# RMSNorm with repeated rows on one core: loads from SyncE and stores from ScalarE, two hardware DMA queues in place of one

## The chip, the cores and the metric

The kernel runs on one core of one Trainium2 chip. The metric is the device time of one execution in microseconds (us); lower is better. An execution more than 1.5% above the fastest of its kernel counts as slow and is left out of the ratios. The rounds of runs fell on several chips, so kernels of different rounds are compared by their ratios to the kernel before, run in the same round. A *load* here is a DMA from HBM to SBUF, a *store* one from SBUF to HBM. SyncE, ScalarE (ACT) and GpSimd (POOL) can issue DMAs; VectorE is DVE. A `q` after an engine's name in a profile line means its sequencer.

## The reference

```python
x: (8, 512, 2048) float32, gamma: (2048,) float32
x_rep = np.repeat(x, 2, axis=1)                       # each row twice
rms = np.sqrt((x_rep ** 2).mean(axis=-1, keepdims=True) + 1e-6)
return (x_rep / rms * gamma).astype(np.float32)       # (8, 1024, 2048)
```

33.6 MB are read and 67.1 MB written, with very little arithmetic per byte.

## The kernel before

The 4096 rows of x are handled in eight tiles of 512 rows, four rows to each of 128 partitions. A tile's buffer `y` holds the output (eight rows per partition); the input is loaded into its upper half. There are three such buffers, so the load of tile i+2 reuses the buffer of tile i-1 and must wait until that tile's store has landed.

```python
K = 4                                           # rows per partition
rows = ctx.enter_context(tc.tile_pool(name="rows", bufs=3))
...                                             # cut
def load(i, parts=1):
    y = rows.tile([P, K * R, D], f32, name="y")
    ...                                         # cut: in `parts` pieces
        nc.sync.dma_start(out=y[:, at : at + step, :], in_=x_t[i, :, k : k + step, :])   # L52
...                                             # cut: load(0), gamma, load(1), load(2)
for i in range(ntiles):
    y = ys[i]
    for k in range(K):
        xk = y[:, K * (R - 1) + k, :]
        y0, y1 = y[:, R * k, :], y[:, R * k + 1, :]
        ...                                     # cut: small tiles
        nc.scalar.activation(out=sq[:], in_=xk, func=Act.Square, accum_out=ss[:])       # L71
        nc.scalar.activation(out=rms[:], in_=ss[:], func=Act.Sqrt, ...)                 # L73
        nc.vector.reciprocal(out=rstd[:], in_=rms[:])                                   # L75
        nc.vector.scalar_tensor_tensor(out=y0, in0=xk, scalar=rstd[:], in1=gamma_b[:], ...)  # L76
        if k == K - 1:
            nc.vector.tensor_copy(out=y1, in_=y0)                                       # L81
        else:
            nc.scalar.copy(out=y1, in_=y0)                                              # L83
    nc.sync.dma_start(out=out_t[i], in_=y.rearrange("p j d -> p (j d)"))                # L84
    if i >= 1 and i + 2 < ntiles:
        load(i + 2)
```

Of the kernel before, what the change touches and what calls it, by code (L numbers as in the profile page):

```python
# [1 line left out]

# [4 lines left out]


@with_exitstack
def kernel(  # L10
    ctx: ExitStack,
    tc: tile.TileContext,
    x: bass.AP,
    gamma: bass.AP,
    out: bass.AP,
):
    nc = tc.nc
    P = nc.NUM_PARTITIONS
    f32 = mybir.dt.float32
    Act = mybir.ActivationFunctionType  # L20
    Alu = mybir.AluOpType

    B, S, D = x.shape
    Bo, So, Do = out.shape
    R = So // S
    assert R == 2 and D == Do and B == Bo and So == S * R
    eps = 1e-6
    inv_d = 1.0 / float(D)


    K = 4
    N = B * S
    assert N % (P * K) == 0
    ntiles = N // (P * K)
    x_t = x.rearrange("b s d -> (b s) d").rearrange("(n p k) d -> n p k d", p=P, k=K)
    out_t = out.rearrange("b s d -> (b s) d").rearrange("(n p j) d -> n p (j d)", p=P, j=K * R)

    singles = ctx.enter_context(tc.tile_pool(name="singles", bufs=1))
    rows = ctx.enter_context(tc.tile_pool(name="rows", bufs=3))
    junk = ctx.enter_context(tc.tile_pool(name="junk", bufs=1, space=bass.MemoryType.PSUM))  # L40
    small = ctx.enter_context(tc.tile_pool(name="small", bufs=8))

    ys = []

    def load(i, parts=1):


        y = rows.tile([P, K * R, D], f32, name="y")
        step = K // parts
        for k in range(0, K, step):  # L50
            at = K * (R - 1) + k
            nc.sync.dma_start(out=y[:, at : at + step, :], in_=x_t[i, :, k : k + step, :])  # L52
        ys.append(y)

    load(0, parts=K)
    gamma_b = singles.tile([P, D], f32, name="gamma_b")
    nc.scalar.dma_start(out=gamma_b[0:1, :], in_=gamma.partition_broadcast(1))
    nc.gpsimd.partition_broadcast(out_ap=gamma_b[:], in_ap=gamma_b[0:1, :])  # L58
    eps_t = singles.tile([P, 1], f32, name="eps_t")
    nc.vector.memset(eps_t, eps)  # L60
    load(1)
    load(2)
# [6 lines that stand above are left out]
            sq = junk.tile([P, D], f32, name="sq")  # L69
            ss = small.tile([P, 1], f32, name="ss")  # L70
            nc.scalar.activation(out=sq[:], in_=xk, func=Act.Square, accum_out=ss[:])  # L71
            rms = small.tile([P, 1], f32, name="rms")
            nc.scalar.activation(out=rms[:], in_=ss[:], func=Act.Sqrt, scale=inv_d, bias=eps_t[:])  # L73
            rstd = small.tile([P, 1], f32, name="rstd")
            nc.vector.reciprocal(out=rstd[:], in_=rms[:])  # L75
            nc.vector.scalar_tensor_tensor(  # L76
                out=y0, in0=xk, scalar=rstd[:], in1=gamma_b[:],
                op0=Alu.mult, op1=Alu.mult,
            )
            if k == K - 1:  # L80
                nc.vector.tensor_copy(out=y1, in_=y0)  # L81
            else:
                nc.scalar.copy(out=y1, in_=y0)  # L83
        nc.sync.dma_start(out=out_t[i], in_=y.rearrange("p j d -> p (j d)"))  # L84
        if i >= 1 and i + 2 < ntiles:
            load(i + 2)


# [1 line left out]
_INS = ['x', 'gamma']  # L90
_OUTS = [((8, 1024, 2048), 'float32')]


# [23 lines left out]
```

## Time and profile before

| | before |
|---|---|
| time, median of the first 3 runs | 240.29 us (239.80 to 241.39) |
| span of the profiled run | 239.1 us |
| DMA queue q1, share of 16 engines | 98.3% |
| ACT busy, DVE busy | 49%, 37% |

These lines of the page show the span, the DMA engines' busy tenths in 40 slices of 6 us, the one queue that carries the traffic, and, for each group of DMA issues, the issuing sequencer, the count, the size and the median time from issue to landing.

```profile
span 239.1 us, 293 instructions
...
DMA  7999998989899999899898999899989899898984
...
q1 hardware_dynamic: 2736, 100.66, 98.3%
...
y<-in_x_dram SPq DMA_DIRECT2D x7, 4096.0 KB, 38.8
...
out_dram<-y SPq DMA_DIRECT2D x8, 32.0
```

The DMA engines are the limit: no slice between the first and the last is below 8. Next, SyncE's own waits (who waited for whom: total us, times, longest):

```profile
SPq L84 <- DVE y L81: 161.7, 8, 28.9
SPq L52 <- DMA out_dram<-y: 38.8, 5, 18.4
```

SyncE has nothing else to do, so it stands at each store (L84) until VectorE's last copy of the tile (L81) is done, and issues it at once. Five loads (L52) wait for the landing of the store that frees their buffer. The end of the run in the timeline (start, duration, engine, line, operation; in brackets the idle time before it and what ended it):

```profile
185.41 1.23 DVE L81 COPY y<-y 128x2048 f32<-128x2048 f32 x1
186.70 0.33 SPq L84 DMA_DIRECT2D out_dram<-y  x1
199.38 1.88 ACT L71 ACTIVATE sq<-y 128x2048 f32<-128x2048 f32 x1 [14.53 <-DMA y<-in_x_dram]
...
215.97 0.33 SPq L84 DMA_DIRECT2D out_dram<-y  x1
```

Tile 6 is done at 186.6 us and its store is issued at 186.70; the last load lands at 199.38, when ACT begins tile 7.

For the accounting below I added up the durations of all packet records of the trace (packets of 8 KB and more, without the queue that loads instructions) and divided by 16. The span is then this sum plus the engines' mean idle time: before, 239.07 = 234.81 + 4.26.

### The profile page before, as it was taken

The numbers are of one execution on the slowest core, as the hardware profiler recorded it, in microseconds if no ns is written. First come the engines' busy times: TensorE is split into PE (matmuls) and PEld (weight loads), VectorE is DVE, ScalarE is ACT, GpSimd is POOL, SyncE is SP. The second block draws the span as 40 slices with busy tenths as digits, with TensorE's granted clock in tenths as the row PEclk, the third lists the DMA queues.
The fourth block names the chain that finished last, engine by engine and source line by source line (L and its number), as shares of the span: only waits on it lengthen the run. The fifth ranks groups of instructions, "written<-read, shape, count | busy, mean of one in ns | idle before, by whom it ended". The sixth has DMA issues, their size and how long they took to land.

```text
span 239.1 us, 293 instructions
## 1 busy us (share of the span) xinstructions
DVE 88.8 (37%) x73; ACT 116.3 (49%) x122; POOL 2.5 (1%) x5
## 2 busy tenths in 40 slices
DVE  0449759590000085400863016820168202591000
ACT  2998999950000299104990059800598006970000
POOL 4000000000000000000000000000000000000000
DMA  7999998989899999899898999899989899898984
GB/s 262 426 454 439 439 439 351 526 351 526 351 428 439 493 395 451 384 411 510 362 515 351 439 439 506 373 422 433 493 384 471 362 461 461 384 482 384 493 384 175
DMA packets 2741, 100.69 MB, mean 421 GB/s; under 512 B 306, under 2 KB 306, under 8 KB 306
## 3 DMA queue, kind: packets, MB, share of 16 engines
q1 hardware_dynamic: 2736, 100.66, 98.3%
q14 instruction: 3, 0.02, 0.0%
q10 hardware_dynamic: 2, 0.01, 0.0%
HBM read 33.56 MB, written 67.11 MB: 421 GB/s over the span
## 4 chain that ended last, share of the span: by engine, by line
DMA 68%; ACT 13%; DVE 8%; SPq 1%; issue 1%
DMA y<-in_x_dram 41%; DMA out_dram<-y 27%; ACT sq L71 7%; DVE y L76 6%; ACT y L83 5%; DVE y L81 2%; SPq L52 1%; ACT rms L73 1%; DVE rstd L75 0%; SPq L84 0%
## 5 line engine op out<-in xcount | busy, mean ns | idle before, releaser
L71 ACT ACTIVATE sq<-y 128x2048 f32<-128x2048 f32 x32 | 59.7, 1865 | 92.5 <-DMA y<-in_x_dram 92.5
L76 DVE SCALAR_TENSOR_TENSOR y<-y,rstd,gamma_b 128x2048 f32<-128x2048 f32 x32 | 75.3, 2352 | 1.2
L75 DVE RECIPROCAL rstd<-rms 128x1 f32<-128x1 f32 x32 | 5.1, 159 | 124.8 <-ACT rms L73 124.8
L83 ACT COPY y<-y 128x2048 f32<-128x2048 f32 x24 | 44.7, 1890 | 3.2 <-DVE y L76 3.2
L81 DVE COPY y<-y 128x2048 f32<-128x2048 f32 x8 | 9.8, 1226 | 0.3
L73 ACT ACTIVATE rms<-ss,eps_t 128x1 f32<-128x1 f32 x32 | 9.4, 293 | 0.7
L71 ACT ACTIVATION_READ_ACCUMULATOR sq<-y 128x1 f32 x32 | 6.0, 186 | 0.0
L58 POOL PARTITION_BROADCAST gamma_b<-gamma_b x1 | 2.3, 2293 | 2.1 <-DMA gamma_b<-in_gamma_dram 2.1
L71 ACT ACT_TABLE_LOAD x1 | 1.3, 1283 | 1.3 <-PEq L101 1.3
L73 ACT ACT_TABLE_LOAD x1 | 1.3, 1283 | 0.0
L60 DVE MEMSET eps_t<- 128x1 f32 x1 | 0.1, 59 | 0.8 <-PEq L101 0.8
L101 POOL MEMSET const-bfloat16-1.0<- 128x1 bf16 x1 | 0.1, 101 | 0.0
L101 POOL MEMSET const-uint8-127<- 128x1 uint8 x1 | 0.1, 101 | 0.0
L101 POOL MEMSET const-float32-0.0<- 128x1 f32 x1 | 0.1, 98 | 0.2 <-issue 0.2
L101 POOL MEMSET const-float32-1.0<- 128x1 f32 x1 | 0.1, 99 | 0.0
## 6 DMA issues: line engine op xcount, KB each, us to landing
y<-in_x_dram SPq DMA_DIRECT2D x7, 4096.0 KB, 38.8
y<-in_x_dram SPq DMA_DIRECT2D x4, 1024.0 KB, 8.0
out_dram<-y SPq DMA_DIRECT2D x8, 32.0
gamma_b<-in_gamma_dram ACTq DMA_DIRECT2D x1, 8.0 KB
```

Of the source, the lines that this page charges most:

```text
L52: nc.sync.dma_start(out=y[:, at : at + step, :], in_=x_t[i, :, k : k + step, :])
L58: nc.gpsimd.partition_broadcast(out_ap=gamma_b[:], in_ap=gamma_b[0:1, :])
L60: nc.vector.memset(eps_t, eps)
L71: nc.scalar.activation(out=sq[:], in_=xk, func=Act.Square, accum_out=ss[:])
L73: nc.scalar.activation(out=rms[:], in_=ss[:], func=Act.Sqrt, scale=inv_d, bias=eps_t[:])
L75: nc.vector.reciprocal(out=rstd[:], in_=rms[:])
L76: nc.vector.scalar_tensor_tensor(out=y0, in0=xk, scalar=rstd[:], in1=gamma_b[:], op0=Alu.mult, op1=Alu.mult,)
L81: nc.vector.tensor_copy(out=y1, in_=y0)
L83: nc.scalar.copy(out=y1, in_=y0)
L101: nc = _bacc.Bacc("TRN2", target_bir_lowering=False, num_devices=1)
```

## The change

The intent: loads wait for buffers and stores wait for compute, so give each its own queue, and neither stands behind the other. The Trainium skill gives this advice ("Perfetto Trace Analysis", DMA Optimizations: one engine for inputs and another for outputs "may make sense").

```diff
-        nc.sync.dma_start(out=out_t[i], in_=y.rearrange("p j d -> p (j d)"))
+        nc.scalar.dma_start(out=out_t[i], in_=y.rearrange("p j d -> p (j d)"))
         if i >= 1 and i + 2 < ntiles:
             load(i + 2)
```

## The prediction

> **What bounds the kernel now.** The DMA engines. In the page's queue part one queue, q1, carries 100.66 MB and its packets take 98.3% of sixteen engines' span (239.1 us). ACT is busy 49%, DVE 37%. Loads are 4 MB in 32 KB packets, stores 8 MB in 64 KB packets. In the trace's packet records the median load packet took 1213 ns, the median store packet 2418 ns: 27.0 and 27.1 GB/s per engine, 432 and 434 GB/s over sixteen. Both directions run alike, so I read this as the engine's own limit. The Trainium skill ("DMA: Bandwidth & Descriptors", Where 436 GB/s comes from) puts the ceiling at 435.2 GB/s; the trace agrees within 1%.
>
> Floor, an estimate from those packets: (512 x 309 ns + 896 x 1213 ns + 1024 x 2418 ns) / 16 = 232.6 us. The records sum to 234.8 us. The other 4.3 us of the span are start and last completion. So at most 2.2 us of stretched packets lie open to a reordering.
>
> **What the change does.** It removes nothing: same bytes, packets and engines. Eight stores leave SyncE (332 ns each) for ScalarE. The same page (Issuing engines are not separate DMA queues) says that such DMAs interleave on the same engines and save only issue time, which is not on the critical path here. In SyncE's waits, 161.7 us go to the last VectorE copy of a tile and 38.8 us (5 times) to a store landing before a load. All five late loads are held by the landing of the store that frees their buffer, not by their place behind a store on SyncE. A second queue cannot issue them earlier.
>
> **What moves.** In one queue the order is strict: store, load, store, load, one pair per 29.2 us (load issues at 101.4, 130.5, 159.7 us in the timeline). With two queues a load and the next store share the engines. If they alternate packet by packet, both finish together some 29 us after the load's issue: loads land after 20 to 30 us instead of 38.8, stores after 35 to 45 us instead of 32. Buffers come free at the same pace.
>
> Does it run dry? A tile computes in about 16.5 us (111.1 to 127.6 us). Before, the last load lands at 199.4, the last store is issued at 216.0, and the store ahead of it needs until about 219: some 3 us to spare. After, I work out the last load landing at 196 to 198 us, its store ready at 213 to 215, the previous store ending at about 216. Still full, with 2 to 3 us to spare; a later last load would cost its excess directly.
>
> ScalarE pays 8 x 0.33 us for issues and waits for VectorE's copy (1.2 us) before the next tile's squares: about 1.7 us per tile, where tiles follow without a gap. It has 92.5 us of waits for loads to absorb it.
>
> **Prediction.** 240 us, unchanged. 8 in 10: 237.8 to 242.5. Faster by over 2%: 0.04 (needs 235.5, below floor plus start and end). Within 2%: 0.90. Slower by over 2%: 0.06.
>
> **What would show it.** Queue part: q1 keeps about 33.6 MB, a ScalarE queue takes 67.1 MB; their shares sum to 97 to 99%. Mean stays 418 to 425 GB/s. Late loads land 20 to 30 us after issue. SyncE's waits are nearly all for stores landing. No slice of the DMA row between start and end falls below 8.
>
> **What would make it wrong.** Faster, if two queues on one engine overlap reads and writes and move more than 27.1 GB/s. Slower, if switching between reads and writes stretches the packets, or if stores starve the last load and the queue runs dry before the last store.

## The result, and the profile after

| | before | after |
|---|---|---|
| median | 240.07 us (4 runs) | 250.18 us (4 runs) |
| ratio | | 1.043, interval 1.036 to 1.050 |
| span of the profiled run | 239.07 us | 248.05 us |
| packet durations / 16 | 234.81 us | 238.05 us |
| DMA engines' mean idle time | 4.26 us | 10.00 us |

A ratio is the mean time of one kernel's fast runs over that of the other's of the same rounds, so it is not quite the ratio of the medians. The change is slower by 4%. The 9.0 us of the span are 5.7 us of idle DMA engines and 3.2 us of packets that took longer.

The page after, the lines that answer to those of before:

```profile
span 248.0 us, 297 instructions
...
DMA  7999999999899899999998989999989947797993
...
q10 hardware_dynamic: 1154, 67.12, 62.5%
q1 hardware_dynamic: 1584, 33.56, 33.5%
...
y<-in_x_dram SPq DMA_DIRECT2D x7, 4096.0 KB, 20.8
...
out_dram<-y ACTq DMA_DIRECT2D x8, 28.4
```

The traffic split as intended. But in the slice from 198 to 205 us (the 4 ahead of 7797993) the DMA engines are 4 tenths busy, and the two next are at 7. In the packet records no packet at all is in flight from 202.8 to 207.7 us. SyncE's wait line is also as foretold:

```profile
SPq L52 <- DMA out_dram<-y: 159.3, 5, 39.8
```

SyncE now waits for buffers only. What went wrong is on ScalarE. The timeline after, around the second to last store:

```profile
178.21 2.35 DVE L76 SCALAR_TENSOR_TENSOR y<-y,rstd,gamma_b 128x2048 f32<-128x2048 f32 x1
203.15 1.88 ACT L71 ACTIVATE sq<-y 128x2048 f32<-128x2048 f32 x1 [25.17 <-DMA y<-in_x_dram]
...
205.39 1.86 ACT L71 ACTIVATE sq<-y 128x2048 f32<-128x2048 f32 x1
205.51 0.16 DVE L75 RECIPROCAL rstd<-rms 128x1 f32<-128x1 f32 x1 [24.95 <-ACT rms L73]
205.59 1.21 DVE L81 COPY y<-y 128x2048 f32<-128x2048 f32 x1
206.72 2.35 DVE L76 SCALAR_TENSOR_TENSOR y<-y,rstd,gamma_b 128x2048 f32<-128x2048 f32 x1
206.84 0.34 ACTq L84 DMA_DIRECT2D out_dram<-y  x1
```

Read this slowly. The last multiplication of tile 6 ends at 180.6 us (178.21 + 2.35). All that its store still lacks is one copy of 1.2 us, on a VectorE that is idle. But the copy (L81) starts at 205.59, behind the first reciprocal of tile *7*, and the store is issued at 206.84, behind the first two squares of tile *7*. Those wait for tile 7's load, which lands at 203.15. The builder's scheduler has put a tile's last copy and its store behind the next tile's first instructions. In the kernel before, the scheduler left the copy ahead of the next tile's reciprocal, and the store was on SyncE, where no compute could stand ahead of it. ScalarE and VectorE issue in order (the Trainium skill, "PSUM — Partial Sum Buffer", Engine vs sequencer instructions, calls their queues "strict FIFO"; this trace agrees: the copy could have run at 180.6 us and ran at 205.6). So every store from tile 1 to tile 6 waits for the load of the next tile. For most of the run the other queue has work meanwhile. At the end no load is left to do so, and the engines run dry.

The ten microseconds around the gap in the view by windows (from and to in us, length, busy us of DVE, ACT and POOL with counts, clock, DMA share, GB/s), for the kernel before:

```profile
200.00:205.00 5.00, 3.19 (x4) 4.94 (x7) 0.00 (x0) 1.00 0.97 419
205.00:210.00 5.00, 2.08 (x3) 5.00 (x6) 0.00 (x0) 1.00 1.00 433
```

and the same view of the changed kernel:

```profile
200.00:205.00 5.00, 0.00 (x0) 1.85 (x2) 0.00 (x0) 1.00 0.35 151
205.00:210.00 5.00, 3.55 (x3) 3.25 (x6) 0.00 (x0) 1.00 0.49 210
```

The DMA share falls from 0.97 and 1.00 to 0.35 and 0.49. (A packet seems to be booked where it starts, so the windows are a little early and a neighbour can show more than 1; the idle sums above are from the packet records.)

### The profile page after: what moved, and what is told of

Its sections match the earlier page's. It is cut to its first block, busy times and chain, and to the rows that moved or that the text cites. A ratio compares the mean times of both kernels' runs of the same rounds, so it can differ in the third digit from the quotient of the medians.

```text
span 248.0 us, 297 instructions
## 1 busy us (share of the span) xinstructions
DVE 88.5 (36%) x73; ACT 115.9 (47%) x122; POOL 2.5 (1%) x5
## 4 chain that ended last, share of the span: by engine, by line
DMA 72%; ACT 11%; DVE 4%; SPq 1%; issue 1%
DMA y<-in_x_dram 48%; DMA out_dram<-y 25%; ACT sq L71 7%; ACT y L83 3%; DVE y L76 3%; DVE y L81 1%; SPq L52 1%; ACT rms L73 1%; DVE rstd L75 0%
## 5 line engine op out<-in xcount | busy, mean ns | idle before, releaser
L81 DVE COPY y<-y 128x2048 f32<-128x2048 f32 x8 | 9.7, 1214 | 0.1
## 6 DMA issues: line engine op xcount, KB each, us to landing
y<-in_x_dram SPq DMA_DIRECT2D x7, 4096.0 KB, 20.8
```

## The experiments

My theory, *O* (order): each store is issued late because it stands behind instructions that wait for the next load. The rivals: *S*, loads and stores that share the engines through two queues cost the time; *A*, ScalarE pays for issuing. The order of instructions was set by adding order-only dependencies at build time; no wait was taken away. In e2 and e12 some lines of the source moved as well. All kernels gave correct results.

| run | issue of stores | ratio to before (interval) | profiled span = packets + idle, us |
|---|---|---|---|
| before | SyncE, in order | 1 | 239.07 = 234.81 + 4.26 |
| the change | ScalarE, late | 1.043 (1.036 to 1.050) | 248.05 = 238.05 + 10.00 |
| after_again | the same | 1.039 (1.035 to 1.043) | 249.03 = 238.46 + 10.56 |
| e1_in_order | ScalarE, in order | 1.009 (1.003 to 1.015) | 241.84 = 234.74 + 7.09 |
| e2_one_queue_late | SyncE, late | 1.016 (1.011 to 1.021) | 243.37 = 234.67 + 8.70 |
| e3_last_in_order | ScalarE, late but for tile 6 | 1.021 (1.015 to 1.027) | 244.03 = 238.14 + 5.90 |
| e4_pool | GpSimd, in order | 1.005 (0.999 to 1.011) | 239.95 = 234.38 + 5.57 |
| e5_vector_order_only | ScalarE, late | 1.034 (1.031 to 1.037) | 248.29 = 238.52 + 9.77 |
| e7_split_last | ScalarE, in order; last tile in 4 parts from SyncE | 1.003 (0.996 to 1.010) | 242.43 = 236.45 + 5.98 |
| e8_half_packets | ScalarE, in order, 32 KB packets | 0.996 (0.993 to 0.999) | 239.42 = 234.83 + 4.59 |
| e10_late_half_packets | ScalarE, late, 32 KB packets | 1.037 (1.033 to 1.040) | 248.36 = 242.13 + 6.23 |
| e11_one_queue_half_packets | SyncE, in order, 32 KB packets | 1.002 (1.000 to 1.005) | 238.94 = 235.10 + 3.84 |
| e12_half_late | ScalarE, first half in order, second half late, 32 KB packets | 0.995 (0.991 to 0.999) | 238.48 = 235.02 + 3.45 |

### e1_in_order: two queues, the old order

`behind(a, key)` adds an order-only edge that keeps `a` after the instruction noted under the key, on the same engine. The diff is against the changed kernel; arguments are cut.

```diff
-            nc.scalar.activation(out=sq[:], ...)
+            s_ = nc.scalar.activation(out=sq[:], ...)
+            if k == 0:
+                behind(s_, 'store')          # next tile's first square: behind this tile's store
-            nc.vector.reciprocal(out=rstd[:], in_=rms[:])
+            r_ = nc.vector.reciprocal(out=rstd[:], in_=rms[:])
+            if k == 0:
+                behind(r_, 'copy')           # next tile's first reciprocal: behind this tile's copy
-                nc.vector.tensor_copy(out=y1, in_=y0)
+                last['copy'] = nc.vector.tensor_copy(out=y1, in_=y0)
-        nc.scalar.dma_start(out=out_t[i], ...)
+        last['store'] = nc.scalar.dma_start(out=out_t[i], ...)
```

> Stores stay on ScalarE, loads on SyncE; only the instruction order is put back to that of the kernel before (VectorE: the tile's last copy ahead of the next tile's first reciprocal; ScalarE: the store ahead of the next tile's first square). Theory O (order): the 9 us come from each store being issued only after the NEXT tile's load has landed, because its copy and its issue stand behind that tile's first instructions on in-order engines; so here about 240 us (238.5 to 242), no idle gap of the DMA near 205 us. Rival S (sharing): two queues with loads and stores on the same engines cost the time; so still about 249 to 250. Rival A (ScalarE pays for issuing): also still about 249.

Measured: median 244.15 us of four runs, one of them slow (248.64); 1.009 times before. The gap at 203 us is gone, and the packets are back to 234.74 us. The timeline shows the store of tile 6 right behind its copy again, 15 us ahead of tile 7's first square:

```profile
187.32 1.23 DVE L95 COPY y<-y 128x2048 f32<-128x2048 f32 x1
188.64 0.34 ACTq L98 DMA_DIRECT2D out_dram<-y  x1
203.40 1.88 ACT L81 ACTIVATE sq<-y 128x2048 f32<-128x2048 f32 x1 [16.63 <-DMA y<-in_x_dram]
...
220.01 0.34 ACTq L98 DMA_DIRECT2D out_dram<-y  x1
```

This supports O against S and A: the same queues and the same issuing engine, with the order alone changed, give back most of the loss. But 2.8 us of idle time remain. The last load lands at 203.40, not at 199.38 as before, so the last store is issued at 220.01, when the one ahead of it has all but drained (in the packet records at most one engine is at work from 217 to 220.8 us). e7 and e8 look into that.

### e2_one_queue_late: one queue, the new order

The diff is against the kernel before.

```diff
             r_ = nc.vector.reciprocal(out=rstd[:], in_=rms[:])
+            if k == 0 and late:
+                late.pop()(r_)               # finish the tile before
...                                           # cut
+        def finish(after=None, i=i, y=y, y0=y0, y1=y1):
+            c_ = nc.vector.tensor_copy(out=y1, in_=y0)
+            ...                              # order-only edge: c_ behind `after`
+            nc.sync.dma_start(out=out_t[i], ...)
+            if i >= 1 and i + 2 < ntiles:
+                load(i + 2)
+        if 1 <= i < ntiles - 1:
+            late.append(finish)
+        else:
+            finish()
```

> One queue as before (all DMAs from SyncE), but on VectorE the last copy of tiles 1 to 6 is placed behind the next tile's first reciprocal, as in the changed kernel, so that the store is late. The scheduler also moves SyncE's order to load, load, store, store. Theory O: slower than before without any second queue, by one idle gap of about 5 us between the last load's landing and the second to last store: 245 us (243 to 248). Rivals S and A: no second queue and no issue on ScalarE, so 240 as before.

Measured: 245.26 us, 1.016 times before, with all four runs within 0.6 us. The page's DMA row has the hole at the same place (the 3 ahead of 8989793 is the slice from 195 to 201 us; a packet seems to be booked where it starts, so a hole shows a little early), with no second queue and no store on ScalarE:

```profile
DMA  7999999998979998979798999797989938989793
```

In the packet records nothing is in flight from 198.0 to 203.0 us. The timeline around it, from the landing of the last load to the late copy and the late store:

```profile
198.45 1.88 ACT L72 ACTIVATE sq<-y 128x2048 f32<-128x2048 f32 x1 [30.20 <-DMA y<-in_x_dram]
...
200.89 1.21 DVE L87 COPY y<-y 128x2048 f32<-128x2048 f32 x1
...
202.16 0.33 SPq L94 DMA_DIRECT2D out_dram<-y  x1
```

The late order by itself costs 4.4 us of idle time. (SyncE's own order changed with it, to two loads and then two stores, as the expectation says; the run does not part the two.) The packets are not stretched (234.67 us), unlike in the changed kernel, so with one queue the late order did not stretch them.

### e3_last_in_order: the order mended for the last two tiles only

The diff is against e1.

```diff
-            if k == 0:
+            if k == 0 and i == ntiles - 1:      # both order-only edges of e1, only here
```

> The changed kernel with the order mended only between the last two tiles. Theory O, with the time lost in the one gap of about 5.7 us after the last load has landed: 244 us (242.5 to 246); the remaining 3 to 4 us would be the stretched load packets at the turn from loads to stores. Rivals S and A: 249 to 250, as only one of eight stores moves.

Measured: 246.15 us, 1.021 times before. Moving one store (issued at 182.0 instead of 206.8 us) removes the 5 us gap and about half of the loss:

```profile
181.96 0.34 ACTq L98 DMA_DIRECT2D out_dram<-y  x1
```

What stays is what the expectation named: the packets sum to 238.14 us, 3.3 more than before.

### e4_pool: stores from GpSimd

```diff
-        nc.scalar.dma_start(out=out_t[i], ...)
+        nc.gpsimd.dma_start(out=out_t[i], ...)
```

> Stores from GpSimd, which does nothing else at that time; loads from SyncE; the order on VectorE and ScalarE is that of the kernel before. Theory O: about 240 us (238 to 243), as stores are issued as soon as the tile is ready, unless descriptors made in software cost something of their own. Rival S: 249 or so, because loads and stores still share the engines through two queues. Rival A: 240.

Measured: 243.32 us median of four runs, one of them slow (253.49); 1.005 times before. Here VectorE and ScalarE keep the order of the kernel before, unforced:

```profile
q0 software_dynamic: 1152, 67.11, 64.6%
...
186.79 1.23 DVE L81 COPY y<-y 128x2048 f32<-128x2048 f32 x1
188.56 0.53 POOL L84 DMA_DIRECT2D out_dram<-y  x1 [28.65 <-DVE y L81]
200.49 1.88 ACT L71 ACTIVATE sq<-y 128x2048 f32<-128x2048 f32 x1 [14.26 <-DMA y<-in_x_dram]
```

Two queues share the engines as in the change, though the page calls GpSimd's queue `software_dynamic` and not `hardware_dynamic`, and the loss is gone within the interval. Together with e1, which keeps the two queues of the change, this refutes S as the cause of the 4%. A small idle gap before the last store remains (216.9 to 218.7 us), as in e1.

### after_again and e5_vector_order_only: which engine's order?

e5 is the changed kernel with only the `behind(r_, 'copy')` edge of e1.

> The changed kernel once more, so that it shares its runs of the kernel before with the next three. Both theories: 1.04 times before.

> The changed kernel with only VectorE's order put back; on ScalarE the store still stands behind the next tile's first two squares. Theory O as now refined (it is the issue on ScalarE, behind a square that waits for the next load, that makes the store late): nothing gained, 1.035 to 1.045 times before. If the place of VectorE's copy were the cause: 1.01 as with both orders mended.

Measured: the changed kernel again 250.69 us, 1.039; e5 249.87 us, 1.034. In e5 the copy of tile 6 is in time again, but the store still stands behind tile 7's first square:

```profile
186.40 1.23 DVE L93 COPY y<-y 128x2048 f32<-128x2048 f32 x1
205.04 1.88 ACT L81 ACTIVATE sq<-y 128x2048 f32<-128x2048 f32 x1 [21.26 <-DMA y<-in_x_dram]
...
207.08 0.34 ACTq L96 DMA_DIRECT2D out_dram<-y  x1
```

(The expectation had it behind two squares; here the second starts at 207.27, after the issue.) With VectorE's copy in time, nearly nothing is gained. The store's place in ScalarE's order is enough to cause the loss.

### e7_split_last and e8_half_packets: the rest of e1

e7 is e1 with the last tile's store cut into four 2 MB parts, each issued from SyncE when its rows are done. e8 is e1 with each store issued as two halves, four of a partition's eight output rows each, back to back (the diff is against e1):

```diff
-        last['store'] = nc.scalar.dma_start(out=out_t[i], in_=y.rearrange("p j d -> p (j d)"))
+        H = K * R // 2
+        for h in (H, 0):
+            st = nc.scalar.dma_start(out=out_t[i, :, h * D : (h + H) * D], in_=y[:, h : h + H, :]...)
+            if h == 0:
+                behind(st, 'store')
+            last['store'] = st
```

> The in-order version, with the last tile's store cut into four rows' parts, each issued from SyncE as soon as its rows are done. It tests what is left of 2.7 us (241.8 against 239.1 us in the profiles) of the in-order version: if it is the gap of about 3 us between the second to last store's end (218 us) and the last store's issue (220.0 us), because the last load shares the engines with a store and lands at 203.4 instead of 199.4 us, the gap is filled and the time is that of before (0.995 to 1.003). If it is a cost of sharing spread over the run, it stays at 1.007 to 1.011.

> The in-order version, with each store issued as two halves, back to back, whose packets are 32 KB instead of 64 KB (as large as the load's). If two queues take turns packet by packet, a load now gets half the engines instead of a third: late loads land about 20 to 23 us after issue instead of 32.5, the last load lands before 199 us, the gap before the last store is gone, and the time is that of before (0.995 to 1.004). If the shares don't follow the packet size, loads still take about 32 us and the time stays near 1.009.

e7 measured 1.003, inside the first expectation but with an interval (0.996 to 1.010) that spans both. Its profile fell on a run of 244.21 us while two others took 241.04 and 241.08, and the fourth, 245.17, counts as slow. In the profile the gap is filled, but the packets took 1.6 us more than in the kernel before, and the idle time is 1.7 us more, with 4.4 us of it in the last 6 us (before: 2.6). I count it as inconclusive for the time, and as a yes for the gap.

e8 is clear: 240.33 us, 0.996 times before. Its page:

```profile
DMA  6999999999999999999999999999999999999993
...
y<-in_x_dram SPq DMA_DIRECT2D x7, 4096.0 KB, 23.6
```

The loads of e1's page, for comparison:

```profile
y<-in_x_dram SPq DMA_DIRECT2D x7, 4096.0 KB, 32.5
```

Late loads land 23.6 us after issue instead of 32.5 us in e1, and the last load lands at 194.0 us instead of 203.4. So the turn of a queue is a packet. The packet records of the changed kernel show it directly: from 31 to 40 us each engine runs one 32 KB load packet of 1.21 us, then one 64 KB store packet of 2.42 us, and so on in turn. The load gets a third of the engines against 64 KB store packets and half against 32 KB ones. The Trainium skill ("DMA: Bandwidth & Descriptors", Queues, rings and completion order) has the round robin between queues at packet granularity; this trace agrees, with one such record per turn.

The 0.996 is not due to the packets alone, as the one-queue version shows:

```diff
-        nc.sync.dma_start(out=out_t[i], in_=y.rearrange("p j d -> p (j d)"))
+        for h in (H, 0):                     # e11: the kernel before, its stores halved as in e8
+            st = nc.sync.dma_start(out=out_t[i, :, h * D : (h + H) * D], in_=y[:, h : h + H, :]...)
```

> One queue as before, order as before, only the stores cut into two halves with 32 KB packets. It tells whether the 0.996 of the in-order two-queue version with halves comes from the packets (then 0.996 here too) or from the second queue (then 1.000 here, 0.998 to 1.003). My own expectation: 1.000 to 1.004, because per byte a 32 KB packet took 1213 ns against 1209 ns for half a 64 KB one.

Measured: 240.61 us, 1.002 times before (1.000 to 1.005).

### e10_late_half_packets and e12_half_late: why some packets were stretched

e10 is e8 without its order edges on the squares and reciprocals, so that the late order of the change is back, with 32 KB packets.

> The changed kernel with its late order kept (the store still behind the next tile's first two squares on ScalarE), but each store issued as two halves whose packets are 32 KB. Worked out by hand: the load of a pair lands about 20 us after issue, some 10 us before the store it shares with, so the late issue 4 us after that landing still comes before the store queue is empty; the gap before the second to last store is gone. If a late issue hurts only where the queue runs empty: 1.00 times before (0.995 to 1.01). If lateness costs by itself, or two queues do: 1.03 to 1.04 as the changed kernel.

Measured: 249.43 us, 1.037. My expectation of 1.00 failed; the time is the one that I had put down for lateness, or two queues, costing by itself (1.03 to 1.04). The gap at 203 us is indeed gone (0.04 us idle from 198 to 212 us, against 5.3 us in the change), but the time went elsewhere: packets that normally take 1.213 us took up to 3.0 us, 9.0 us per engine over their usual lengths in all. In the kernel before, this excess is 2.2 us, in the changed kernel 5.5 us, in e8 1.7 us. In time, the excess of the changed kernel sits at four moments beyond those that every run has: from 80 to 84, 88 to 92, 140 to 144 and 148 to 152 us. These follow a load's issue at 80.7 and 141.3 us, when the store queue had just run empty, and the next store's late issue at 85.5 and 146.4 us onto the empty queue. So two of the four are at a load: at 81.6 and 142.3 us, when the engines had just run out of packets (0.75 us of idle time at each), the load's first packet on most engines took 1.5 to 2.2 us in place of 1.21. The other two are the load packet on each engine just ahead of the store's first one, of about 2.1 us. The odd tiles' late stores (105.2 and 165.7 us), issued while another store was still under way, show no such excess. One stretched load packet per engine stands ahead of the first store of every run, too, with one queue as with two (before: at 30.4 us, about 2.2 us long), so a second queue is not the only way to it.

So I guessed that the excess comes with a store that starts on a queue that is empty or nearly so, not with lateness as such. e12 keeps half of each store just as late, and issues the other half in order:

```diff
+        last['first'] = half(0, 'sq')        # rows 0 and 1: ahead of the next tile's first square
+        def second(i=i, half=half):
+            half(H, 'sq')                    # rows 2 and 3
+            ...                              # cut: the load of tile i+2
+        if 1 <= i < ntiles - 1:
+            late.append(second)              # called behind the next tile's second square
+        else:
+            second()
```

(`half` issues the store of half a tile.)

> The late version with halves failed its prediction: its gap before the second to last store was gone, but its packets took 9.0 us more per engine than their usual length (in-order with halves: 1.7 us), most of it within some 8 us after a late store's issue. Here the second half of each store is exactly as late (behind the next tile's second square on ScalarE), but the first half is issued in order, so that the store queue is never empty when the next tile's compute and the late issue come. If the stretching comes from a store that starts on a queue that is empty or about to be: packets stretched by 1.5 to 2.7 us as in order, and 0.995 to 1.006 times before. If it comes from issuing DMAs late, next to the next tile's compute or next to the load's issue: stretched by 8 to 9 us and 1.03 times before.

Measured: 239.90 us, 0.995 times before. The excess fell to 1.9 us and the idle time to 3.45 us, although a half-store is issued at 79.1 us behind tile 3's second square, just ahead of a load at 82.6 us, and so on for each tile:

```profile
78.90 1.86 ACT L82 ACTIVATE sq<-y 128x2048 f32<-128x2048 f32 x1
...
79.08 0.34 ACTq L102 DMA_DIRECT2D out_dram<-y  x1
...
82.65 0.33 SPq L63 DMA_DIRECT2D y<-in_x_dram  x1
```

This agrees with the guess and not with lateness or nearness to compute. (VectorE's last copy is in time in e12 and late in e10, but e5 has it in time and keeps an excess of 5.9 us.) It is one arrangement, and the guess does not cover all of e10: some 2.2 us of its excess come about 16 us after a late store's issue, at 96, 128, 160 and 192 us. *Why* packets of a running queue slow down when another queue starts afresh, the runs don't show; that stays open.

## Why the prediction was wrong

The prediction was 240.0 us, 237.8 to 242.5; measured 250.18 us.

- **What bounds the kernel: right.** The DMA engines bound it, and the floor of 232.6 us holds in every run. The section that the prediction cites for 435.2 GB/s gives this as the ceiling of the fabric, and says that between HBM and SBUF a lower limit of HBM binds, about 358 GB/s; the 421 GB/s of the kernel before are above that.
- **Sharing is free: nearly right.** With the stores in order, e1 (1.009), e4 (1.005) and e8 (0.996) share the engines through two queues at a cost of at most about 1.5% (the upper ends of the intervals are 1.015, 1.011 and 0.999). This also agrees with the Trainium skill ("DMA: Bandwidth & Descriptors", Issuing engines are not separate DMA queues).
- **The step that failed** is this sentence: "ScalarE pays 8 x 0.33 us for issues and waits for VectorE's copy (1.2 us) before the next tile's squares: about 1.7 us per tile, where tiles follow without a gap. It has 92.5 us of waits for loads to absorb it." It takes for granted that the store stands *ahead of* the next tile's squares, as in the source. In the built kernel it stands behind two of them. The 92.5 us of waits for loads, which I booked as slack that would absorb the cost, became waits in front of the store: tile 6's store was issued at 206.8 us, where e3 could issue it at 182.0. Put in order (e1), the same change costs 0.9% instead of 4%.
- **The queue running dry: named, for the wrong reason.** The prediction listed "the queue runs dry before the last store" as a risk, by way of a late last load. That also exists, as e1 shows: the last load landed at 203.4 us, not at the predicted 196 to 198, and cost 2.8 us of idle time. But the larger gap lay one store earlier.
- **Signs that told:** the two shares summed to 96.0% (97 to 99 expected), the mean was 406 GB/s (418 to 425), and between start and end one slice fell to 4 and three to 7 (none below 8). Late loads landed after 20.8 us in the median (20 to 30), which was right and said nothing of the trouble.
- **Stretched packets: named as a risk, but given no time.** The prediction had "if switching between reads and writes stretches the packets"; they made 3.2 of the 9.0 us. Switching alone is not the condition: the kernel before takes loads and stores in turn all through, with 2.2 us of excess in all. Beyond the excess at the first store that every run has, it came with late stores in a second queue that was empty or nearly so (the change, e3, e5, e10), and not with lateness alone (e2) or a second queue alone (e1, e4, e8). That the empty queue is the condition rests on e12; the longer packets in the one profiled run of e7 are unexplained.

## What to carry to other kernels

A DMA issued from a compute engine is an instruction in that engine's in-order stream: ask what stands ahead of it in the *built* order, and what that waits for. An engine's idle time is slack only for work that stands ahead of the wait, not for work behind it. If two queues are to share the DMA engines, keep the store queue from running empty and make the packets of both alike; here that gave 0.996 and 0.995 of the time before, so even at its best the second queue was worth half a per cent. (That the empty queue is what to avoid is the guess that e12 supports, not a proven rule.)

## What the Trainium skill lacked or had wrong

- "Perfetto Trace Analysis", DMA Optimizations, advises one engine for inputs and another for outputs without the condition that decided here: on ScalarE the stores stood behind squares that wait for loads, and the kernel became 4% slower (1.043); with the order mended 1.009.
- "DMA: Bandwidth & Descriptors", Issuing engines are not separate DMA queues, says that issuing from several engines only saves issue time. The engines' bandwidth was indeed the same, but the section lacks that two queues change each transfer's share, which the round robin by packet lets one expect: late loads landed after 32.5 us beside 64 KB store packets and after 23.6 us beside 32 KB ones, which moved the last load by 9 us.
- The same page, Queues, rings and completion order, speaks of a packet of about 9 to 17 descriptors as the turn of a queue. In these traces the turn was one record of 32 or 64 KB, one partition's contiguous run; how many descriptors a record holds they don't show, so this adds a size in bytes and contradicts nothing.
- No page that I read has the cost of starting a queue afresh while transfers of the other kind are on their way: in the change about 0.6 to 1 us of every engine's time at each of four moments, two at a load and two at a late store, and 9.0 us of stretched packets in e10 against 1.7 us in e8.
